# Moving GpSimd's elementwise work to VectorE, and projecting the pooling branch first, in a decoder step on one core

## The chip, the core and the metric

The kernel runs on one core of a Trainium2 chip, in one launch. The core's engines work side by side and wait for each other by semaphores: TensorE (PE in the profile; PEld is its loading of weights), VectorE (DVE), ScalarE (ACT), GpSimd (POOL) and SyncE (SP), which issues most of the DMAs. Each engine executes its own queue strictly in order, so an instruction that waits holds up everything behind it. The metric is the time of an execution in device microseconds; lower is better.

## The reference

Two layers work on 256 prompt tokens and 8 sample tokens (264 columns), with d = 1024. Each layer is a half-step feed-forward block, a mixer and a second half-step feed-forward block. Cut to what the change touches:

```python
def modulate(x, g, shift, scale):
    return rms_norm(x, g) * (1 + scale) + shift
def swiglu(h, w1, w2):
    gate, up = split(h @ w1);  return (silu(gate) * up) @ w2
def pool_mixer(u, ...):       # 4 channel groups of 64, windows w = 2, 4, 8, 16
    d = (c - c_prev) / min(w, pos + 1) - u          # c: running sums
    return concat(d @ pool_w[g]) * pool_scale
def merge_out(...):
    a = o.reshape(b, s, ATTN_WIDTH) @ w_oa          # attention branch, 768 wide
    p = pool_y @ w_op                               # pooling branch, 256 wide
    return (sigmoid(ga) * a + sigmoid(gp) * p) @ w_out
```

The 8 sample tokens attend to cached keys and values, 55 per head over three head groups, and that is done elementwise (multiply, then reduce), not on TensorE.

## The kernel before

**Exact products from a fast format.** Each weight and each activation is split into a high part in the fast format (`whi`, `h_hi`, `ah`) and the rest (`wlo`, `h_lo`, `al`). A block of 128x128 weights is three matmuls on 264 columns: high x high, low x high, high x low (`block`, `mm`, L495 to L508). ScalarE casts `whi`, VectorE subtracts to get `wlo`, in pieces of 128x512 for four blocks; at most some 24 blocks ahead of TensorE.

**Normalisation** (`norm_mod`, L461). After a stage's last product VectorE works out the row factors, scales eight chunks (`ht`, `h_scale`), ScalarE adds the shift and casts (`h_hi`, `h_shift`), and the low part is the difference (`h_lo`). Chunks 1, 3 and 5 (`ON_POOL`) get theirs on GpSimd in two operations, the other five on VectorE in one. The next stage's first two output chunks start in `mm_late` (L510): first the 32 matmuls that need `h_hi`, then the 16 that need `h_lo` (L521), those of GpSimd's chunks last. This happens five times after the start: before each mixer, and before each feed-forward block but the first.

**The mixer** (L592). 36 output chunks of the input projection run on TensorE; in between come the matmuls of attention. `prompt` does four rounds (two halves of the tokens, two head parities): scores into PSUM (`sc`, L779), biased on VectorE (`s`, L785), row maxima (`pnm`), exponentials on ScalarE, transposes, product with V (`oo`). `sample` does the 8 sample tokens: GpSimd multiplies the cached keys by q in four pieces (`kv`, L699), VectorE reduces; after the softmax GpSimd multiplies the values (L741), VectorE reduces into `os`; two masked copies `zo` go to TensorE (L755), whose result `oh`, `ol` completes the operands of the output projection. The pieces go through two buffers: piece i+2 is loaded by SyncE when piece i is reduced. `pooling` (L839) builds windowed sums on GpSimd (`sa`, `sb`) and three small operations for the samples on VectorE (`sm`).

**Order.** The program is written with a planner, class `Clock`: small generators (`spawn`) are resumed when the planned time, advanced by each block of TensorE's work (`tick`), reaches what they yield; `V.done()`, `A.done()` and `G.done()` are planned ends of an engine's queue, from a price per instruction that knows nothing of other engines. `clock.drain()` runs all that is left before the program goes on. So a change of engine changes the order in which TensorE's small matmuls stand among the large ones.

**Output** (L949). For each of eight chunks TensorE does 6 blocks of the attention branch (`pa`) and 2 of the pooling branch (`pp`), after the drain; VectorE multiplies each by its gate `tg`, GpSimd adds the two, ScalarE casts, GpSimd subtracts; then comes the product with `w_out`.

Of the kernel before, what the change touches and what calls it, by code (L numbers as in the profile page):

```python
# [18 lines left out]
KC = 8  # L19
# [15 lines left out]
          (61, 63, 65, 67, 69, 71, 73, 75), (95, 98, 101, 104, 107, 110, 113, 116), ())  # L35

ON_POOL = (1, 3, 5)

# [166 lines left out]
def decoder_step_kernel(ctx: ExitStack, tc: tile.TileContext, wts, ada0, ada, xin, first_in, consts_in, sel_in,  # L205
# [304 lines left out]
    def mm_late(chunks, ops):  # L510


        n = len(ops)
        held = []
        for k, (ah, al) in enumerate(ops):
            for ps, b in chunks:
                held.append((k in ON_POOL, k, ps, block(ps, b + k, ah, k == 0), al))

        held.sort(key=lambda v: v[:2])
        for _, k, ps, wh, al in held:  # L520
            nc.tensor.matmul(ps, wh, al, start=False, stop=(k == max(ON_POOL)))  # L521
        clock.tick(0.34 * n * len(chunks))
        return chunks[-1][1] + n
# [21 lines left out]
    def ffn(l, i, b, h, nxt):  # L545
        hh, hl = h
        with tc.tile_pool(name="ffn", bufs=1) as fp:
# [44 lines left out]
    def mixer(l, b, h):  # L592
# [82 lines left out]
        def sample():  # L675
# [60 lines left out]
            for i, (gs, s0, n) in enumerate(PIECES):  # L736
                yield from kv_wait()
                vv = kv.pop(0)[0].rearrange("p (d s) -> p d s", s=n)
                for g, a0, n_ in gs:
                    w = vv[:, :, a0:a0 + n_]  # L740
                    G.tensor_tensor(w, w, p55[:, s0 + a0:s0 + a0 + n_].unsqueeze(1).to_broadcast([P, 64, n_]),  # L741
                                            op=OP.mult)
                yield G.done()
                for g, a0, n_ in gs:
# [94 lines left out]
        def pooling():  # L839
# [3 lines left out]
            n = n16  # L843
            gp = G
            u = rows[:, 12:14]
            us = u[:, :, NP:NT]
            for i, w in enumerate((2, 4, 8, 16)):
# [3 lines left out]
            gp.memset(sa[:, :, 0:16], 0.0)  # L851
            gp.memset(sb[:, :, 0:16], 0.0)
            gp.tensor_copy(sa[:, :, 16:17], u[:, :, 0:1])
            gp.tensor_tensor(sa[:, :, 17:n], u[:, :, 1:NP], u[:, :, 0:NP - 1], op=OP.add)
            gp.tensor_tensor(sb[:, :, 16:n], sa[:, :, 16:n], sa[:, :, 14:n - 2], op=OP.add)
            gp.tensor_tensor(sa[:, 1, 16:n], sb[:, 1, 16:n], sb[:, 1, 12:n - 4], op=OP.add)
            gp.tensor_tensor(sb[64:, 1, 16:n], sa[64:, 1, 16:n], sa[64:, 1, 8:n - 8], op=OP.add)
            for c in range(2):
                for r, src in ((0, sa), (64, sb)):
                    cnt = cc[r:r + 64, C_CNT + c * 16:C_CNT + c * 16 + 16]  # L860
                    gp.tensor_tensor(sa[r:r + 64, c, 16:32], src[r:r + 64, c, 16:32], cnt, op=OP.mult)
                    gp.tensor_scalar(sa[r:r + 64, c, 32:n], src[r:r + 64, c, 32:n],
                                     cc[r:r + 64, C_IW + c:C_IW + c + 1], None, op0=OP.mult)
# [19 lines left out]
            clock.hold("sc", V)  # L883

        def start():
# [31 lines left out]
        for j in range(36):  # L917
# [23 lines left out]
            else:  # L941
                while j == 30 and st["scored"] < 4:
                    clock.tick(0.2)
                A.activation(tg[:, j - 20], ps, AF.Tanh, scale=0.5)
        clock.drain()
        ax.close()


        with tc.tile_pool(name="out", bufs=1) as op_:  # L949
# [3 lines left out]
            def merged(m):  # L953
                G.tensor_tensor(tg[:, m], tg[:, m], tg[:, 8 + m], op=OP.add)
                yield G.done()
                A.copy(mh[:, m], tg[:, m])
                yield A.done()
                G.tensor_tensor(ml[:, m], tg[:, m], mh[:, m].bitcast(F32), op=OP.subtract)

            for m in range(KC):  # L960
                pa = acc_tile()
                b = mm(pa, b, [(oh[:, k], ol[:, k]) for k in range(6)])
                pp = acc_tile()
                b = mm(pp, b, [(ph[:, k], pl[:, k]) for k in range(2)])
                V.scalar_tensor_tensor(tg[:, m], tg[:, m], 1.0, pa, op0=OP.add, op1=OP.mult)
                V.scalar_tensor_tensor(tg[:, 8 + m], tg[:, 8 + m], 1.0, pp, op0=OP.add, op1=OP.mult)
                clock.spawn(merged(m), V.done())
            mops = [(mh[:, k], ml[:, k]) for k in range(KC)]
# [122 lines left out]
def _constants():  # L1091
# [16 lines left out]
    for k in range(2):  # L1108
        for half in range(2):
            w = 2 ** (2 * k + half + 1)  # L1110
            cnt = np.minimum(w, np.arange(16) + 1)
            o = C_CNT + k * 16
            c[64 * half:64 * half + 64, o:o + 16] = (np.float32(1) / cnt.astype(np.float32))[None]
            c[64 * half:64 * half + 64, C_IW + k] = 1.0 / w
# [149 lines left out]
```

## Time and profile before

| What | Value |
|---|---|
| time, median of 3 runs | 1268.76 us (1268.53 to 1269.59) |
| the profiled execution | 1268.73 us, its span 1267.0 us |
| TensorE busy | 1240.2 us, 98% |
| VectorE, ScalarE, GpSimd busy | 809.8, 550.6, 207.0 us |
| mean granted clock of TensorE | 0.993 |
| chain that ended last | PE 91%, DVE 7% |

The span is the time from the first instruction to the last of one execution. TensorE's matmuls are pipelined and their ends are modelled, so "busy" covers small delays between matmuls; what a stage loses is read from the starts of its matmuls in the timeline. The granted clock is 1.00 at the higher of TensorE's two levels and 0.50 at the lower. Durations of neighbouring VectorE instructions overlap by some hundredths of a microsecond, so a run of them ends earlier than their sum.

### The profile page before, as it was taken

Reading aid. Unit: us, or ns where it says so; the run is one execution under the profiler, and the core shown is the slowest. Engines: PE = TensorE matmul, PEld = TensorE weight load, DVE = VectorE, ACT = ScalarE, POOL = GpSimd, SP = SyncE. Lnnn points to the kernel's source line nnn. Section 1 sums busy time; section 2 is a strip of 40 time slices with the busy share of each in tenths; the row PEclk is TensorE's granted clock in tenths of the full one; section 3 lists DMA queues with packets and bytes.
Section 4 is the critical chain, followed back from the end, with each engine's and each line's share of the span. In section 5 each row is a group of like instructions: output and inputs, shape, how many; then the busy total and the mean of one; then the engine's idle time right before and its main releaser. Section 6 shows DMA issues by size and latency. Waiting matters only on the chain.

```text
span 1267.0 us, 25911 instructions
## 1 busy us (share of the span) xinstructions
PE 1240.2 (98%) x10866; PEld 1176.0 (93%) x10866; DVE 809.8 (64%) x1533; ACT 550.6 (43%) x850; POOL 207.0 (16%) x218
## 2 busy tenths in 40 slices
PE   8999999999999999999999999999999999999998
PEld 6999999989899979999989999998997998999998
DVE  4555554676887775556567565557489878666653
ACT  2344333355453544344434444344555444544431
POOL 0012110010423321111002111001014251111100
PEclk9999999999898999999999999999999999999999
DMA  9688887555257737679745677763732784887652
GB/s 391 264 300 312 303 331 282 202 202 200 68 214 267 258 132 262 231 284 388 267 165 177 253 302 294 288 249 124 278 133 94 281 308 158 318 288 291 233 174 101
DMA packets 41989, 306.27 MB, mean 242 GB/s; under 512 B 4928, under 2 KB 6208, under 8 KB 8640
## 3 DMA queue, kind: packets, MB, share of 16 engines
q1 hardware_dynamic: 41248, 303.02, 64.8%
q8 instruction: 85, 1.39, 0.4%
q0 software_dynamic: 336, 1.29, 0.3%
q10 hardware_dynamic: 288, 0.30, 0.1%
q14 instruction: 32, 0.26, 0.1%
HBM read 299.73 MB, written 26.03 MB: 257 GB/s over the span
## 4 chain that ended last, share of the span: by engine, by line
PE 91%; DVE 7%; DMA 1%; issue 1%; ACT 0%; POOL 0%; DVEq 0%; SPq 0%; ACTq 0%; POOLq 0%
PE mm L497 27%; PE mm L498 26%; PE mm L506 26%; PE pa L286 3%; DVE ht L133 2%; PE mm L521 1%; PE oo L1072 1%; PE sc L779 1%; DMA wraw<-in_wts_dram 1%; DVE wlo L133 1%; DVE h_lo L133 1%; PE tr L807 1%; DVE sm L133 1%; PE oo L819 1%; PE pa L1012 1%
## 5 line engine op out<-in xcount | busy, mean ns | idle before, releaser
L133 DVE TENSOR_TENSOR wlo<-wraw,whi 128x512 fp32r<-128x512 f32 x736 | 547.5, 775 | 280.8 <-ACT whi L133 278.7
L497 PE MATMUL mm<-h_hi,whi 128*128 128x264 f32 x2088 | 600.9, 290 | 4.4 <-ACT h_hi L133 3.1
L133 ACT CAST whi<-wraw 128x1024 fp32r<-128x1024 f32 x368 | 384.8, 1049 | 489.1 <-PE mm L506 222.8
L498 PE MATMUL mm<-h_hi,wlo 128*128 128x264 f32 x2088 | 589.5, 284 | 0.0
L506 PE MATMUL mm<-h_lo,whi 128*128 128x264 f32 x1952 | 554.2, 284 | 0.0
L497 PEld LDWEIGHTS mm<-h_hi,whi 128*128 128x128 f32 x2088 | 394.7, 189 | 27.5 <-issue 15.8
L498 PEld LDWEIGHTS mm<-h_hi,wlo 128*128 128x128 f32 x2088 | 395.0, 189 | 0.0
L506 PEld LDWEIGHTS mm<-h_lo,whi 128*128 128x128 f32 x1952 | 367.3, 188 | 0.0
L498 PE MATMUL mm<-ah,wlo 128*128 128x264 f32 x704 | 201.1, 286 | 0.0
L506 PE MATMUL mm<-al,whi 128*128 128x264 f32 x704 | 200.2, 284 | 0.0
L497 PE MATMUL mm<-ah,whi 128*128 128x264 f32 x704 | 199.7, 284 | 0.0
L133 POOL TENSOR_TENSOR al<-fa,ah 128x264 fp32r<-128x264 f32 x88 | 89.6, 1019 | 495.3 <-ACT ah L133 494.0
L497 PEld LDWEIGHTS mm<-ah,whi 128*128 128x128 f32 x704 | 133.1, 189 | 2.5 <-issue 1.6
L498 PEld LDWEIGHTS mm<-ah,wlo 128*128 128x128 f32 x704 | 132.3, 188 | 0.0
L506 PEld LDWEIGHTS mm<-al,whi 128*128 128x128 f32 x704 | 132.1, 188 | 0.0
L133 DVE TENSOR_TENSOR fa<-fsi,mm 128x264 f32<-128x264 f32 x86 | 36.7, 427 | 71.1 <-PE mm L506 71.1
L133 POOL TENSOR_TENSOR ht<-ht,mods 128x256 f32<-128x256 f32 x15 | 11.1, 741 | 263.9 <-ACT h_hi L133 263.9
L133 ACT ACTIVATE h_hi<-ht,mods 128x256 fp32r<-128x256 f32 x48 | 22.6, 504 | 59.3 <-DVE ht L133 49.1
L133 DVE SCALAR_TENSOR_TENSOR x<-mm,mods,x 128x256 f32<-128x256 f32 x48 | 23.1, 481 | 39.4 <-PE mm L506 39.2
L286 PE MATMUL pa<-wraw,fc 128*32 128x256 f32 x544 | 36.4, 385 | 0.0
L133 ACT CAST ah<-fa 128x264 fp32r<-128x264 f32 x88 | 35.9, 409 | 0.6 <-DVE fa L133 0.6
L133 ACT ACTIVATE fsi<-mm 128x264 f32<-128x264 f32 x87 | 33.4, 383 | 0.5 <-PE mm L1036 0.3
(178 smaller groups left out, 947.9 us busy)
## 6 DMA issues: line engine op xcount, KB each, us to landing
wraw<-in_wts_dram SPq DMA_DIRECT2D x184, 1024.0 KB, 5.3
wraw<-in_ada_dram SPq DMA_DIRECT2D x34, 1024.0 KB, 5.8
araw<-in_ada_dram SPq DMA_DIRECT2D x30, 1024.0 KB, 7.3
a<-in_ada_dram SPq DMA_DIRECT2D x2, 2048.0 KB, 14.4
a<-in_ada_dram SPq DMA_DIRECT2D x4, 1024.0 KB, 22.4
out_og_dram<-in_cg_dram SPq DMA_DIRECT2D x2, 2032.0 KB, 10.4
out_rows_dram<-rows SPq DMA_DIRECT2D x2, 1848.0 KB, 10.8
kv<-in_ksamp_dram SPq DMA_DIRECT2D x8, 416.0 KB, 3.8
```

The source lines that it names most:

```text
L133: return f(*a, **k)
L286: nc.tensor.matmul(pa[32 * c:32 * c + 32], sc_t[:, 2 * q + r], t[:, r, c], start=(q + r == 0), stop=(q == 3 and r == 1), tile_position=(0, ...
L497: nc.tensor.matmul(ps, wh, ah, start=first, stop=False)
L498: nc.tensor.matmul(ps, wl, ah, start=False, stop=False)
L506: nc.tensor.matmul(ps, wh, al, start=False, stop=(k == n - 1))
L521: nc.tensor.matmul(ps, wh, al, start=False, stop=(k == max(ON_POOL)))
L779: nc.tensor.matmul(sc[e][:, i], qn[r:r + 64, c, q0:q0 + 128], rows[r:r + 64, c, 0:nk * 128], start=True, stop=True, tile_position=(r, 0))
L807: nc.tensor.transpose(pt[:, i], sf[:, k0:k0 + 128], ident)
L819: nc.tensor.matmul(po[64 * e:64 * e + 64, g], st["vt"][:, kt, h_ * 64:h_ * 64 + 64], s[e][:, g, kt * 128:kt * 128 + 128], start=(kt == 0), ...
L1012: nc.tensor.matmul(pa[32 * c:32 * c + 32], sc_t[:, r], t[:, r, c], start=(r == 0), stop=(r == KC - 1), tile_position=(0, 32 * c))
L1072: nc.tensor.matmul(pw, wr[:, 0:P], wr[:, 0:n], start=True, stop=True)
```

## The change

All two-tensor operations of GpSimd go to VectorE: the low parts of the three chunks in the normalisation (now the same one operation as the others; `mm_late` has no late chunks any more), the low parts `al` in the feed-forward blocks, the multiplications of the sample's keys and values, the windowed sums, and the merge of the branches. GpSimd keeps memsets and a few DMAs. Pooling multiplies by 1/w and subtracts the token in one operation; the counts of the first 16 positions are scaled by w to fit. The eight `pp` chunks are computed ahead of the drain, right after the input projection, and the weights lie in that order; after the drain come the eight `pa` chunks.

```diff
@@ norm_mod
-            if m in ON_POOL:
-                G.tensor_tensor(ts[m], ts[m], mods[l][:, 3 * i, m, 0:1].to_broadcast([P, NP]), op=OP.add)
-                G.tensor_tensor(lo[:, m, 0:NP], ts[m], hi[:, m, 0:NP].bitcast(F32), op=OP.subtract)
         next(smp, None)
-        for m in [m for m in range(KC) if m not in ON_POOL]:
+        for m in range(KC):
             h_low(l, i, m, hi, lo, ts[m])
@@ mm_late
-                held.append((k in ON_POOL, k, ps, block(ps, b + k, ah, k == 0), al))
-
-        held.sort(key=lambda v: v[:2])
-        for _, k, ps, wh, al in held:
...
+                held.append((k, ps, block(ps, b + k, ah, k == 0), al))
+        for k, ps, wh, al in held:
...
@@ gated
                 A.copy(ah[:, c], a)
-                G.tensor_tensor(al[:, c], a, ah[:, c].bitcast(F32), op=OP.subtract)
+                yield A.done()
+                V.tensor_tensor(al[:, c], a, ah[:, c].bitcast(F32), op=OP.subtract)
@@ sample (keys; the values change alike)
-                    G.tensor_tensor(kk[:, a0:a0 + n_], kk[:, a0:a0 + n_],
+                    V.tensor_tensor(kk[:, a0:a0 + n_], kk[:, a0:a0 + n_],
                                             sqkv[:, g].unsqueeze(1).to_broadcast([P, n_, 64]), op=OP.mult)
-                yield G.done()
+                yield V.done()
@@ pooling
+            V.tensor_tensor(sa[:, :, 17:n], u[:, :, 1:NP], u[:, :, 0:NP - 1], op=OP.add)
+            yield V.done()
+            V.tensor_tensor(sb[:, :, 16:n], sa[:, :, 16:n], sa[:, :, 14:n - 2], op=OP.add)
+            yield V.done()
...
+            for c in range(2):
+                for r, src in ((0, sa), (64, sb)):
...
+                    V.tensor_tensor(src[r:r + 64, c, 16:32], src[r:r + 64, c, 16:32], cnt, op=OP.mult)
+                    V.scalar_tensor_tensor(sa[r:r + 64, c, 16:n], src[r:r + 64, c, 16:n],
+                                           cc[r:r + 64, C_IW + c:C_IW + c + 1], u[r:r + 64, c, 0:NP],
+                                           op0=OP.mult, op1=OP.subtract)
+                yield V.done()
...
-            gp.tensor_tensor(sa[:, :, 16:n], sa[:, :, 16:n], u[:, :, 0:NP], op=OP.subtract)
-            yield G.done()
@@ mixer, output
+        while not st.get("pool"):
+            clock.tick(0.2)
+        for m in range(KC):
+            pp = acc_tile()
+            b = mm(pp, b, [(ph[:, k], pl[:, k]) for k in range(2)])
+            V.scalar_tensor_tensor(tg[:, 8 + m], tg[:, 8 + m], 1.0, pp, op0=OP.add, op1=OP.mult)
         clock.drain()
...
-                G.tensor_tensor(tg[:, m], tg[:, m], tg[:, 8 + m], op=OP.add)
-                yield G.done()
+                V.tensor_tensor(tg[:, m], tg[:, m], tg[:, 8 + m], op=OP.add)
+                yield V.done()
...
-                G.tensor_tensor(ml[:, m], tg[:, m], mh[:, m].bitcast(F32), op=OP.subtract)
+                V.tensor_tensor(ml[:, m], tg[:, m], mh[:, m].bitcast(F32), op=OP.subtract)
...
-                pp = acc_tile()
-                b = mm(pp, b, [(ph[:, k], pl[:, k]) for k in range(2)])
...
-                clock.spawn(merged(m), V.done())
+                clock.spawn(merged(m))
+                clock.run(clock.t)
```

What the planner makes of it is read from the order of the instructions. First VectorE in the normalisation, before:

```order
L133 SCALAR_TENSOR_TENSOR ht<-x,mods,rb 128x256 x7
L133 TENSOR_TENSOR hs<-hs,mods 128x64
L133 TENSOR_TENSOR h_lo<-hs,h_hi 128x8x8
L133 SCALAR_TENSOR_TENSOR h_lo<-ht,mods,h_hi 128x256 x5
L133 STREAM_TRANSPOSE tt<-pa 128x256
```

and now:

```order
L131 SCALAR_TENSOR_TENSOR ht<-x,mods,rb 128x256 x7
L131 TENSOR_TENSOR hs<-hs,mods 128x64
L131 TENSOR_TENSOR h_lo<-hs,h_hi 128x8x8
L131 SCALAR_TENSOR_TENSOR h_lo<-ht,mods,h_hi 128x256 x8
L131 STREAM_TRANSPOSE tt<-pa 128x256
```

Three `h_lo` join the five, and nothing else moves there. Next VectorE in the attention of layer 0, from the scores of the third round (`s`, the first four of six) to those of the fourth, before:

```order
L133 SCALAR_TENSOR_TENSOR s<-cc,sc 128x256 x4
L133 TENSOR_TENSOR of<-oo,of 128x384
L133 TENSOR_TENSOR wlo<-wraw,whi 128x512
L133 TENSOR_TENSOR sm<-sm,rows 128x16
L133 TENSOR_TENSOR sm<-sm,cc 128x16
L133 TENSOR_TENSOR sa<-sm,rows 128x2x8
L133 SCALAR_TENSOR_TENSOR s<-cc,sc 128x256 x2
L133 TENSOR_REDUCE pnm<-s 128x1 x2
L133 TENSOR_REDUCE s_4048<-kv 128x13
L133 SCALAR_TENSOR_TENSOR s<-cc,sc 128x256 x4
```

and now:

```order
L131 SCALAR_TENSOR_TENSOR s<-cc,sc 128x256 x4
L131 TENSOR_TENSOR sa<-sb 128x256
L131 TENSOR_TENSOR sb<-sa 64x256
L131 TENSOR_REDUCE s_4030<-kv 128x13
L131 TENSOR_TENSOR kv<-kv,sqkv 128x832
L131 TENSOR_TENSOR of<-oo,of 128x384
L131 TENSOR_TENSOR wlo<-wraw,whi 128x512
L131 SCALAR_TENSOR_TENSOR s<-cc,sc 128x256 x2
L131 TENSOR_REDUCE pnm<-s 128x1 x2
```

The three small `sm` operations stand later now, and sums, a reduction and a multiplication stand in their place; on TensorE the fourth round's scores come after 27 large matmuls behind the third's last scores, where 6 stood before. Last TensorE at the end of the sample's attention, before:

```order
L498 MATMUL mm<-h_hi,wlo 128x264
L506 MATMUL mm<-h_lo,whi 128x264
L755 MATMUL tr<-cc,zo 128x16 x3
L497 MATMUL mm<-h_hi,whi 128x264
L498 MATMUL mm<-h_hi,wlo 128x264
```

and now:

```order
L493 MATMUL mm<-ph,wlo 128x264
L501 MATMUL mm<-pl,whi 128x264
L749 MATMUL tr<-cc,zo 128x16 x3
L492 MATMUL mm<-oh,whi 128x264
L493 MATMUL mm<-oh,wlo 128x264
```

The transposes of `zo` stand behind the 48 matmuls of the pooling branch now, and directly ahead of the attention branch, which reads their result; two blocks of the input projection stood between before.

## Rows read from the trace of the kernel before

**Rows 1.** The page, busy time of each engine over the whole span.
```profile
PE 1240.2 (98%) x10866; PEld 1176.0 (93%) x10866; DVE 809.8 (64%) x1533; ACT 550.6 (43%) x850; POOL 207.0 (16%) x218
```

**Rows 2.** Waits of TensorE: us in total, times, longest.
```profile
PE sc L779 <- DVE s L133: 6.2, 2, 3.1
PE tr L755 <- DVE zo L133: 4.1, 2, 2.2
```

**Rows 3.** Timeline of one normalisation: start, us, engine, operation, count, wait in brackets.
```profile
254.30 0.48 DVE L133 SCALAR_TENSOR_TENSOR ht<-x,mods,rb 128x256 f32<-128x256 f32 x1
...
254.81 1.85 ACT L133 ACTIVATE h_hi<-ht,mods 128x256 fp32r<-128x256 f32 x4 [4.88 <-DVE ht L133]
254.83 4.54 DVE L133 SCALAR_TENSOR_TENSOR ht<-x,mods,rb 128x256 f32<-128x256 f32 x7
...
255.37 0.39 PE L497 MATMUL mm<-h_hi,whi 128*128 128x264 f32 x1 [0.55 <-ACT h_hi L133]
...
255.93 0.64 POOL L133 TENSOR_TENSOR ht<-ht,mods 128x256 f32<-128x256 f32 x1 [69.36 <-ACT h_hi L133]
...
260.67 2.06 DVE L133 SCALAR_TENSOR_TENSOR h_lo<-ht,mods,h_hi 128x256 fp32r<-128x256 f32 x5
...
261.19 2.84 PE L521 MATMUL mm<-h_lo,whi 128*128 128x264 f32 x16 [0.48 <-DVE h_lo L133]
```

**Rows 4.** VectorE's groups by shape: busy us, mean ns, idle before.
```profile
L133 DVE TENSOR_TENSOR wlo<-wraw,whi 128x512 fp32r<-128x512 f32 x736 | 547.5, 775 | 280.8 <-ACT whi L133 278.7
...
L133 DVE SCALAR_TENSOR_TENSOR ht<-x,mods,rb 128x256 f32<-128x256 f32 x48 | 28.5, 651 | 0.0
...
L133 DVE SCALAR_TENSOR_TENSOR tg<-tg,mm 128x264 f32<-128x264 f32 x32 | 13.7, 427 | 7.0 <-PE mm L506 6.9
L133 DVE SCALAR_TENSOR_TENSOR s<-cc,sc 128x256 f32<-128x256 f32 x24 | 8.6, 410 | 3.7 <-PE sc L779 3.7
L133 DVE TENSOR_REDUCE s<-kv 128x13 f32<-128x832 f32 x8 | 8.1, 1006 | 0.0
...
L133 DVE TENSOR_REDUCE o<-kv 128x64 f32<-128x576 f32 x2 | 1.5, 742 | 0.0
```

**Rows 5.** Timeline of the score stall, layer 0; the last row is layer 1.
```profile
332.28 1.13 PE L779 MATMUL sc<-rows,tg 64*128 64x256 f32 x8
...
336.43 4.31 POOL L133 TENSOR_TENSOR kv<-kv,sqkv 128x832 f32<-128x832 f32 x2
...
336.94 1.94 DVE L133 TENSOR_TENSOR sm<-sm,rows 128x16 f32<-128x16 f32 x1
...
337.52 0.28 PE L498 MATMUL mm<-h_hi,wlo 128*128 128x264 f32 x1
...
338.01 0.28 PE L506 MATMUL mm<-h_lo,whi 128*128 128x264 f32 x1
341.37 2.40 PE L779 MATMUL sc<-rows,tg 64*128 64x256 f32 x8 [3.08 <-DVE s L133]
...
961.25 2.37 PE L779 MATMUL sc<-rows,tg 64*128 64x256 f32 x8 [3.08 <-DVE s L133]
```

**Rows 6.** Windows: us, busy PE, PEld, DVE, ACT, POOL (count), granted clock, DMA, GB/s.
```profile
340.00:344.00 4.00, 2.63 (x9) 1.98 (x10) 3.97 (x7) 1.40 (x3) 0.74 (x1) 0.55 0.00 0
```

**Rows 7.** Windows of TensorE alone: us, busy (count), granted clock, DMA, GB/s.
```profile
347.00:348.00 1.00, 1.00 (x9) 0.88 1.06 427
401.00:402.00 1.00, 1.00 (x7) 0.57 0.98 418
965.00:966.00 1.00, 1.00 (x10) 0.97 0.83 113
```

**Rows 8.** The key and value tiles: time from issue to landing.
```profile
DMA to landing us min/median/max: 3.3/3.7/7.3
```

**Rows 9.** Timeline where the sample's result reaches TensorE, layers 0 and 1.
```profile
394.78 1.26 PE L755 MATMUL tr<-cc,zo 128*128 128x16 f32 x6 [2.23 <-DVE zo L133]
...
1013.34 0.84 PE L755 MATMUL tr<-cc,zo 128*128 128x16 f32 x6 [1.90 <-DVE zo L133]
```

More of the change, by code (lines that the diff above doesn't have):

```diff
@@ L35 @@
           (61, 63, 65, 67, 69, 71, 73, 75), (95, 98, 101, 104, 107, 110, 113, 116), ())
-ON_POOL = (1, 3, 5)
 FIRST = ((0, 4), (4, 6), (6, 8))
@@ L516, in mm_late @@
             for ps, b in chunks:
-                held.append((k in ON_POOL, k, ps, block(ps, b + k, ah, k == 0), al))
-        held.sort(key=lambda v: v[:2])
-        for _, k, ps, wh, al in held:
-            nc.tensor.matmul(ps, wh, al, start=False, stop=(k == max(ON_POOL)))
+                held.append((k, ps, block(ps, b + k, ah, k == 0), al))
+        for k, ps, wh, al in held:
+            nc.tensor.matmul(ps, wh, al, start=False, stop=(k == n - 1))
         clock.tick(0.34 * n * len(chunks))
@@ L740, in sample @@
                     w = vv[:, :, a0:a0 + n_]
-                    G.tensor_tensor(w, w, p55[:, s0 + a0:s0 + a0 + n_].unsqueeze(1).to_broadcast([P, 64, n_]),
+                    V.tensor_tensor(w, w, p55[:, s0 + a0:s0 + a0 + n_].unsqueeze(1).to_broadcast([P, 64, n_]),
                                             op=OP.mult)
-                yield G.done()
+                yield V.done()
                 for g, a0, n_ in gs:
@@ L843, in pooling @@
             n = n16
-            gp = G
             u = rows[:, 12:14]
             us = u[:, :, NP:NT]
+            G.memset(sa[:, :, 0:16], 0.0)
+            G.memset(sb[:, :, 0:16], 0.0)
+            A.copy(sa[:, :, 16:17], u[:, :, 0:1])
+            V.tensor_tensor(sa[:, :, 17:n], u[:, :, 1:NP], u[:, :, 0:NP - 1], op=OP.add)
+            yield V.done()
+            V.tensor_tensor(sb[:, :, 16:n], sa[:, :, 16:n], sa[:, :, 14:n - 2], op=OP.add)
+            yield V.done()
+            V.tensor_tensor(sa[:, 1, 16:n], sb[:, 1, 16:n], sb[:, 1, 12:n - 4], op=OP.add)
+            V.tensor_tensor(sb[64:, 1, 16:n], sa[64:, 1, 16:n], sa[64:, 1, 8:n - 8], op=OP.add)
+            yield V.done()
+            for c in range(2):
+                for r, src in ((0, sa), (64, sb)):
+                    cnt = cc[r:r + 64, C_CNT + c * 16:C_CNT + c * 16 + 16]
+                    V.tensor_tensor(src[r:r + 64, c, 16:32], src[r:r + 64, c, 16:32], cnt, op=OP.mult)
+                    V.scalar_tensor_tensor(sa[r:r + 64, c, 16:n], src[r:r + 64, c, 16:n],
+                                           cc[r:r + 64, C_IW + c:C_IW + c + 1], u[r:r + 64, c, 0:NP],
+                                           op0=OP.mult, op1=OP.subtract)
+                yield V.done()
             for i, w in enumerate((2, 4, 8, 16)):
@@ L850, in pooling @@
                                         axis=AX.X, op=OP.add)
[L851 to L863, printed above, removed]
-            gp.tensor_tensor(sa[:, :, 16:n], sa[:, :, 16:n], u[:, :, 0:NP], op=OP.subtract)
-            yield G.done()
             V.tensor_tensor(sm, sm, us, op=OP.add)
@@ L883, in pooling @@
             clock.hold("sc", V)
+            st["pool"] = True
         def start():
@@ L953, in merged @@
             def merged(m):
-                G.tensor_tensor(tg[:, m], tg[:, m], tg[:, 8 + m], op=OP.add)
-                yield G.done()
+                V.tensor_tensor(tg[:, m], tg[:, m], tg[:, 8 + m], op=OP.add)
+                yield V.done()
                 A.copy(mh[:, m], tg[:, m])
                 yield A.done()
-                G.tensor_tensor(ml[:, m], tg[:, m], mh[:, m].bitcast(F32), op=OP.subtract)
+                V.tensor_tensor(ml[:, m], tg[:, m], mh[:, m].bitcast(F32), op=OP.subtract)
             for m in range(KC):
@@ L962, in mixer @@
                 b = mm(pa, b, [(oh[:, k], ol[:, k]) for k in range(6)])
-                pp = acc_tile()
-                b = mm(pp, b, [(ph[:, k], pl[:, k]) for k in range(2)])
                 V.scalar_tensor_tensor(tg[:, m], tg[:, m], 1.0, pa, op0=OP.add, op1=OP.mult)
-                V.scalar_tensor_tensor(tg[:, 8 + m], tg[:, 8 + m], 1.0, pp, op0=OP.add, op1=OP.mult)
-                clock.spawn(merged(m), V.done())
+                clock.spawn(merged(m))
+                clock.run(clock.t)
             mops = [(mh[:, k], ml[:, k]) for k in range(KC)]
@@ L1112, in _constants @@
             o = C_CNT + k * 16
-            c[64 * half:64 * half + 64, o:o + 16] = (np.float32(1) / cnt.astype(np.float32))[None]
+            c[64 * half:64 * half + 64, o:o + 16] = (np.float32(w) / cnt.astype(np.float32))[None]
             c[64 * half:64 * half + 64, C_IW + k] = 1.0 / w
@@ L1183 @@
                 stream.append(tiles(blocks(a["w_in"][l], (2, 0, 1, 3))))
-                both = np.concatenate([a["w_oa"][l], a["w_op"][l]], axis=0)
-                stream.append(tiles(blocks(both, (2, 0, 1, 3))))
+                stream.append(tiles(blocks(a["w_op"][l], (2, 0, 1, 3))))
+                stream.append(tiles(blocks(a["w_oa"][l], (2, 0, 1, 3))))
                 stream.append(tiles(blocks(a["w_out"][l], (2, 0, 1, 3))))
```

## The prediction

> **What bounds the kernel now.** I read the page's busy times first: TensorE is busy for 1240.2 of 1267.0 us [rows 1]. So an edit on another engine counts only where TensorE waits for that engine, and the next view is the list of TensorE's waits. Two of its lines are long: the scores `sc` of L779 wait for VectorE's `s`, 3.1 us in each layer, and the transposes of L755 wait for `zo`, 2.2 us at most [rows 2]. The third place hides inside "busy": in the timeline of a normalisation the first pass begins at 255.37 and the second ends at 264.03 [rows 3]. That is 48 matmuls, and a matmul follows the one before by 0.12 us where nothing is in the way (four of them from 337.52 to 338.01 [rows 5]), so 5.8 us of work take 8.5. There are five such places. Of this only what GpSimd's work causes can go.
>
> GpSimd slows VectorE. The first `ht` of the normalisation starts at 254.30 and the next at 254.83 with a small operation between, but seven take 4.54 us, 0.65 each, and they stretch once GpSimd begins at 255.93 [rows 3]; the mean of all 48 is 651 ns, while `s`, as many elements from PSUM and SBUF in the same kind of instruction, takes 410 [rows 4]. It is starker in the attention: `sm`, on 16 elements per partition, takes 1.94 us beside two GpSimd multiplications of 2.15 each [rows 5].
>
> **The change part by part.** All sums are against the profiled execution's 1268.73 us, 1.7 more than its span and practically the median of the runs, 1268.76.
>
> *A, normalisation.* It adds three `h_lo` per place and takes GpSimd away. After the change: seven `ht` from 254.83 at 0.41 (the price of `s`) end at 257.7; two small operations, 0.4 together; eight `h_lo` at 0.41 each, as five take 2.06 when GpSimd has finished [rows 3], end at 261.4. TensorE is through its first pass earlier: 32 matmuls from 255.37, at most one group of four per ScalarE's 0.46 (four in 1.85 [rows 3]) or per 4 x 0.12, whichever is longer, end by 259.4. So the last `h_lo` decides, and with 0.1 us to the two last matmuls and their modelled end of 0.28 the place ends at 261.9 instead of 264.0: 2.1 us. Five times: -10.5. Ends: had the 0.65 nothing to do with GpSimd, the last `h_lo` would come 1.2 us later than now and the six matmuls for GpSimd's chunks (0.7) would no longer trail, +0.5 a place or +2.5; were `ht` as quick as the rows' overlap allows, -12.5.
>
> *B, scores.* Before, the first eight `sc` take 1.13 us [rows 5]; the stalled ones wait 3.08 and take 2.40, since the granted clock stands at 0.55 in 340 to 344 [rows 6]. It comes back at about 347.2 (0.88 in the window from 347 [rows 7]), so the stretch from 343.7 to there, 3.5 us at half the speed, loses 1.8 more. Layer 0 loses 3.08 + 1.27 + 1.8 = 6.1; layer 1 3.08 + 1.24 and, with the clock back at 965.06, half of 1.5: 5.1. After: TensorE reaches these scores at 332.28 + 1.13 + 15 x 0.12 + 0.6 (the third round's last scores, half as many) + 27 x 0.12 + 1.2 (transposes and `oo`: some 19 matmuls of 128 columns, an estimate at half of 0.12) = 340.2. VectorE needs, from the third round's first scores at 333.4: 4 x 0.41, two sums 0.8, a reduction 1.0 and a multiplication as wide 1.0, `of` 0.55 (384 elements, between the 410 ns of 256 and the 742 of 576), a `wlo` 0.78 at most, two `s` 0.8 [rows 4]: 339.9, and some 0.5 less as they overlap. So the wait goes, by a margin of 0.3 to 0.8 us. -11.2; ends 0 (a stall as long elsewhere in the layer) and -11.2.
>
> *C, end of the sample.* Before: 2.23 us of wait, 0.4 on the slowed transposes and half of the 6.0 us to about 401.9 where the clock returns [rows 7, 9], 5.6 in layer 0; layer 1 waits 1.90 and keeps its clock: 7.5 together. After, 48 matmuls of the pooling branch (5.85 us from a point S) stand ahead of the transposes. They look like a cover, but VectorE has no time either. A `wlo` depends on a cast whose buffer TensorE frees, so VectorE can't run ahead, and from the first gate product at about S + 0.8 it has in its queue ahead of the end of `zo`: 7 gate products at 0.43, 3 `wlo` at 0.78, the multiplication and the reduction of the last piece (0.74 + 0.41 each, after the reduction of 576 elements [rows 4] and `s`), and four small ones, an estimate of 0.3 each, below the 0.41 of 256 elements: 8.8, or S + 9.6. The overlap of some 0.07 on 16 operations takes off 1.1: S + 8.5. TensorE is done at S + 6.2: of three accumulators the sixth product needs the one that the third gate product frees at about S + 4.0 (0.8 + 3 x 0.43 + 0.78 + 1.15), and would start at S + 3.65. So it idles 2.3 us again, and 0.55 more because `oh` and `ol` are read at once, with no two blocks between. The clock fell after 2.23 and not after 1.90 [rows 7, 9]; I take one fall of 3.0 us: (2.3 + 0.3 + 0.55) x 2 + 3.0 = 9.3, so +1.8. Ends: no idle, 1.1 - 7.5 = -6.4; 3.4 us of idle with two falls, +7.0.
>
> *At nothing: the feed-forward blocks.* 88 `al` at 0.43 join VectorE. A chunk there is 16 blocks or 48 matmuls, 5.8 us; VectorE needs four `wlo` (3.1), `fa` and `al` (0.9): 4.0. The second product reads the last `al` only in its 22nd block, 8 us on. Without that cover it is 0.5 us a block of feed-forward, four times.
>
> *At nothing: pooling and merge.* Pooling costs VectorE about 4.5 us a layer (two operations of 512 elements at 0.7, six of 256 at 0.41, four of 16 at an estimated 0.2), and by the order its product comes on TensorE 102 large matmuls, 12 us, after the scores above; the merge is one more operation of 0.43 and one subtraction per 18 matmuls. Cover gone, the last merge (1.7 us from product to cast) would show, but `mm_late` reads that chunk only after 28 matmuls, 3.4 us.
>
> *The waits that are added.* The key and value multiplications now wait for their DMAs in VectorE's queue, with scores and `wlo` behind them. A load lands 3.7 us after its issue, 7.3 at most [rows 8], and by the order VectorE has eight or more other operations, some 6 us, between the reduction that frees the buffer and the multiplication. Nothing by the median, 1.3 us by the maximum.
>
> Sum: -10.5 - 11.2 + 1.8 = -19.9, or 1248.8; I say 1249.
>
> VectorE is busy for 3.97 of 4 us while TensorE stalls [rows 6]. The Trainium skill, in "Perfetto Trace Analysis", section "Optimizing Scalar/DVE Operations", says that with a saturated VectorE it may make sense to offload, even to GpSimd, which speaks against this change; the same place warns that the two share a read port and that moving work between them might not help. By the first half the time would be that of the third rival below; the 1.94 us for 16 elements speak for the second half, since much of that 3.97 is waiting.
>
> **The rivals.**
> 1. *The sample is through in time.* The pooling branch hides `zo`, C is -6.4: 1268.7 - 10.5 - 11.2 - 6.4 = 1240.6. For it: 5.85 us of cover. Against: my count of VectorE's queue, unless the operations overlap more.
> 2. *A new stall of the same kind.* The score stall goes, but a round's maxima, or a key multiplication, comes late elsewhere in each layer and brings the clock down: B is nothing, 1260. For it: a margin below 1 us, which one `wlo` more uses up. Against: without GpSimd the planner's prices are near what VectorE takes.
> 3. *VectorE's queue becomes the bound (slower).* Place: the attention, from the first key multiplication to `zo`. It gains eight pieces at 1.0 (as the reductions [rows 4]) and 4.5 of pooling, 12.5 us a layer. If nothing comes back from GpSimd there and VectorE has no slack, TensorE waits for all of it, 25 us: 1268.7 - 10.5 + 25 = 1283. It decides from the point where VectorE lags by more than the 24 blocks, 8.8 us, that `wlo` is ahead. Against: operations of microseconds for 16 elements shrink to 0.2.
> 4. *GpSimd isn't what stretches `ht`.* A is +2.5: 1261.8. Against: the first `ht`.
> 5. *No change.* A and B come only by half and the sample's end costs its upper 7.0: 1268.7 - 5 - 5.6 + 7 = 1265, or with one more stall about 1268.
>
> **How the numbers follow.** Forecast 0.58; rivals in order 0.14, 0.13, 0.07, 0.04, 0.04. The range of 8 in 10 goes from the first rival's time to the second's, 1240 to 1260; the forecast's own is 1244 to 1254. A measurement tells 0.2%, about 2.5 us, from no change. Faster: 0.58 + 0.14 + 0.13 + 0.04 = 0.89; the same 0.04; slower 0.07.
>
> **What the profile after would show.** Right: `ht` at some 0.41 us in the mean; the last matmul of the second pass 6.5 us after the first of the first pass instead of 8.7; no wait of `sc` for `s` in the list, and no low clock there; a wait of the transposes for `zo` of about 2 us in each layer, behind the pooling branch. VectorE's `wlo` shorter than 775 ns. Wrong: `ht` still near 0.65 (then A falls); a wait over 2 us of a `sc`, `tr` or `oo` in the attention; no wait for `zo` (then C was too dear); waits of large matmuls for `wlo` (then the third rival).

## The result and the profile after

The changed kernel takes 1251.76 us (median of 4 runs, 1250.90 to 1252.62), the kernel before 1268.64 beside it: ratio 0.9870, interval 0.9853 to 0.9887. The forecast was 1249, its range 1240 to 1260. The profiled execution took 1250.9 us, span 1249.1.

The page's first lines, to be read beside [rows 1]: GpSimd is all but empty (4.1 us), and VectorE's 1716 instructions, 88 `al` among them, take less time than before.

```profile
span 1249.1 us, 25734 instructions
...
PE 1230.0 (98%) x10866; PEld 1170.8 (94%) x10866; DVE 787.7 (63%) x1716; ACT 548.5 (44%) x852; POOL 4.1 (0%) x16
```

TensorE's waits (total, times, longest), beside [rows 2]: the line of `sc` is gone, that of `zo` has grown, and two short ones are new, for an accumulator (`tg`: its gate product on VectorE frees it) and for `oh`.

```profile
PE tr L749 <- DVE zo L131: 5.0, 2, 2.5
PE mm L492 <- ACT h_hi L131: 3.2, 5, 0.8
...
PE mm L492 <- DVE tg L131: 0.9, 2, 0.5
PE mm L492 <- ACT oh L131: 0.6, 2, 0.3
```

The normalisation of [rows 3]: `ht` runs through, and the second pass no longer waits for `h_lo`.

```profile
254.50 2.86 DVE L131 SCALAR_TENSOR_TENSOR ht<-x,mods,rb 128x256 f32<-128x256 f32 x7
...
257.67 3.25 DVE L131 SCALAR_TENSOR_TENSOR h_lo<-ht,mods,h_hi 128x256 fp32r<-128x256 f32 x8
...
255.04 0.39 PE L492 MATMUL mm<-h_hi,whi 128*128 128x264 f32 x1 [0.56 <-ACT h_hi L131]
259.12 2.37 PE L514 MATMUL mm<-h_lo,whi 128*128 128x264 f32 x16
```

VectorE's groups by shape (busy us, mean ns, idle before), beside [rows 4]: `ht` 651 to 479 ns, `wlo` 775 to 687; `s`, which has one operand in PSUM, stays where it was (410, now 416).

```profile
L131 DVE TENSOR_TENSOR wlo<-wraw,whi 128x512 fp32r<-128x512 f32 x736 | 488.9, 687 | 288.1 <-ACT whi L131 285.7
...
L131 DVE SCALAR_TENSOR_TENSOR ht<-x,mods,rb 128x256 f32<-128x256 f32 x48 | 20.1, 479 | 0.0
...
L131 DVE SCALAR_TENSOR_TENSOR s<-cc,sc 128x256 f32<-128x256 f32 x24 | 8.6, 416 | 2.1 <-PE sc L773 2.1
...
L131 DVE TENSOR_TENSOR sm<-sm,rows 128x16 f32<-128x16 f32 x2 | 0.4, 176 | 0.1
```

The scores of the fourth round, stalled in [rows 5], start without a wait: VectorE's two `s` of the third round, which these scores wait for, end at 337.3, and TensorE comes at 338.94. Counted from the third round's first scores (332.28 before, 330.24 now), the two `s` start after 6.3 us and not 8.6, and TensorE comes after 8.7 us, where it would have come after 6.0 (341.37 less its wait of 3.08). First VectorE before, then the changed kernel:

```profile
340.90 0.74 DVE L133 SCALAR_TENSOR_TENSOR s<-cc,sc 128x256 f32<-128x256 f32 x2
```

```profile
330.24 1.14 PE L773 MATMUL sc<-rows,tg 64*128 64x256 f32 x8
...
336.57 0.74 DVE L131 SCALAR_TENSOR_TENSOR s<-cc,sc 128x256 f32<-128x256 f32 x2
...
338.94 1.14 PE L773 MATMUL sc<-rows,tg 64*128 64x256 f32 x8
```

The window of [rows 6] is full, at full clock.

```profile
340.00:344.00 4.00, 4.00 (x35) 3.99 (x34) 3.99 (x9) 1.99 (x5) 0.00 (x0) 1.00 0.26 57
```

The end of the sample, beside [rows 9]: VectorE first (from 386.77 on, seven gate products `tg` stand ahead of the last reductions and `zo`), then TensorE, which begins the pooling branch at 385.26, has finished it by 392 and waits in both layers.

```profile
386.77 0.76 DVE L131 SCALAR_TENSOR_TENSOR tg<-tg,mm 128x264 f32<-128x264 f32 x2
...
391.62 0.42 DVE L131 SCALAR_TENSOR_TENSOR tg<-tg,mm 128x264 f32<-128x264 f32 x1
391.95 0.75 DVE L131 TENSOR_REDUCE o<-kv 128x64 f32<-128x576 f32 x1
...
393.71 0.73 DVE L131 TENSOR_SCALAR zo<-os,cc 128x192 f32<-128x192 f32 x2
...
385.26 0.28 PE L492 MATMUL mm<-ph,whi 128*128 128x264 f32 x1
...
389.53 0.39 PE L492 MATMUL mm<-ph,whi 128*128 128x264 f32 x1 [0.47 <-DVE tg L131]
...
394.49 0.84 PE L749 MATMUL tr<-cc,zo 128*128 128x16 f32 x6 [2.50 <-DVE zo L131]
395.62 0.48 PE L492 MATMUL mm<-oh,whi 128*128 128x264 f32 x1 [0.29 <-ACT oh L131]
...
1002.40 0.84 PE L749 MATMUL tr<-cc,zo 128*128 128x16 f32 x6 [2.51 <-DVE zo L131]
```

Windows of TensorE alone behind these waits (busy, granted clock, DMA, GB/s): the lower level, 1.2 GHz, in both layers; at this place the kernel before had it in layer 0 alone ([rows 7]).

```profile
396.00:399.00 3.00, 3.00 (x16) 0.50 0.91 289
...
1004.00:1006.00 2.00, 2.00 (x11) 0.50 0.86 233
```

The loads of [rows 8] land in 3.4 us at the median, 6.5 at most, and nothing waits for them.

### The profile page after: what moved, and what is told of

The parts are those of the page before. It is cut to its first block, busy times and chain, and to the rows that moved or that the text cites. A ratio compares the mean times of both kernels' runs of the same rounds, so it can differ in the third digit from the quotient of the medians.

```text
span 1249.1 us, 25734 instructions
## 1 busy us (share of the span) xinstructions
PE 1230.0 (98%) x10866; PEld 1170.8 (94%) x10866; DVE 787.7 (63%) x1716; ACT 548.5 (44%) x852; POOL 4.1 (0%) x16
## 3 DMA queue, kind: packets, MB, share of 16 engines
q8 instruction: 85, 1.39, 0.5%
## 4 chain that ended last, share of the span: by engine, by line
PE 94%; DVE 4%; issue 0%; ACT 0%; POOL 0%; DVEq 0%; ACTq 0%; POOLq 0%
PE mm L492 29%; PE mm L493 28%; PE mm L501 26%; PE pa L284 3%; PE oo L1074 1%; PE mm L514 1%; PE sc L773 1%; PE oo L813 1%; PE tr L801 1%; PE pa L1014 1%; DVE wlo L131 1%; DVE ht L131 1%; DVE h_lo L131 0%; DVE tg L131 0%; DVE o L131 0%
## 5 line engine op out<-in xcount | busy, mean ns | idle before, releaser
L131 DVE TENSOR_TENSOR wlo<-wraw,whi 128x512 fp32r<-128x512 f32 x736 | 488.9, 687 | 288.1 <-ACT whi L131 285.7
L131 DVE TENSOR_TENSOR al<-fa,ah 128x264 fp32r<-128x264 f32 x88 | 37.5, 427 | 0.0
L492 PE MATMUL mm<-oh,whi 128*128 128x264 f32 x96 | 28.9, 301 | 0.6 <-ACT oh L131 0.6
```

The costliest lines, as they stand in the source:

```text
L131: return f(*a, **k)
L492: nc.tensor.matmul(ps, wh, ah, start=first, stop=False)
```

## The experiments

Times are medians; a difference is against the kernel before of the same job (1267.8 to 1268.7 us), or against the changed kernel where said.

**1. The normalisation alone, in the kernel before.**

```
-ON_POOL = (1, 3, 5)
+ON_POOL = ()
-  ... stop=(k == max(ON_POOL)))
+  ... stop=(k == n - 1))
```

> The kernel before with one edit: the low parts of all eight chunks of the normalisation on VectorE (all else as before). Theory (GpSimd's six operations stretch VectorE's there): each of five places takes 6.4 us from the first matmul to the end of the second pass instead of 8.6, ht falls from 651 to about 480 ns, and the time falls by 11 us, to 1257.7. Rival (ht is as slow by itself, so VectorE only gets three operations more): +2.5 us, 1271. The score stall and the waits for zo stay as before under both.

1257.82 us (ratio 0.9928, 0.9915 to 0.9942): 10.4 less. `ht` 479 ns, `wlo` still 775, the wait for `s` as before, those for `zo` 3.1 us in all and not 4.1. Term A stands by itself, at its predicted price.

**2. The changed kernel with GpSimd's six normalisation operations as extra work** on a tile that nothing reads; VectorE's and TensorE's queues hold the same instructions in the same order.

```
+ if m in (1, 3, 5):
+     G.tensor_tensor(sh[:, 0], ts[m], shift, op=OP.add)
+     G.tensor_tensor(sh[:, 1], sh[:, 0], hi[m], op=OP.subtract)
```

> The changed kernel, with GpSimd doing the six operations of the normalisation of before once more into a tile that nobody reads; VectorE's and TensorE's queues are the same, instruction by instruction. Theory (contention with GpSimd): ht goes back to about 650 ns, each of the five places takes 9 us or more instead of 6.4, and the time rises by 13 us, to 1265. Rival (the gain came from the order of the instructions or from no longer waiting for GpSimd's results): nothing waits for the tile, so the time stays within 1 us of 1251.8.

1266.24 us, 14.5 more than the changed kernel. In the timeline `ht` is back at its old pace though nobody waits for GpSimd:

```profile
254.85 4.55 DVE L131 SCALAR_TENSOR_TENSOR ht<-x,mods,rb 128x256 f32<-128x256 f32 x7
255.65 0.95 POOL L131 TENSOR_TENSOR shadow<-ht,mods 128x256 f32<-128x256 f32 x1 [252.99 <-ACT h_hi L131]
...
260.69 3.25 DVE L131 SCALAR_TENSOR_TENSOR h_lo<-ht,mods,h_hi 128x256 fp32r<-128x256 f32 x8
261.21 3.07 PEld L518 LDWEIGHTS mm<-h_lo,whi 128*128 128x128 f32 x16 [0.69 <-DVE h_lo L131]
```

So GpSimd's mere activity stretches `ht`; rival 4 is out. From the first matmul to the end of the second pass the five places take 45.1 us together instead of 32.0, which is 13.1 of the 14.5 us. That is more than A because eight `h_lo`, not five, now follow the stretched `ht`.

**3. The changed kernel with extra GpSimd work in the attention**: five additions of 384 elements behind each key multiplication, unread.

```
+ G.tensor_tensor(sh, kk[:, 0:6], fc, op=OP.add)
+ for _ in range(4): G.tensor_tensor(sh, sh, fc, op=OP.add)
```

> The changed kernel, with five GpSimd additions of 384 elements behind each of the four key multiplications, into a tile that nobody reads; VectorE's and TensorE's queues are unchanged. GpSimd is then busy for some 5 us behind each piece, about as it was around the score stall before. Theory (the stall of 3.1 us came from VectorE being held by GpSimd): VectorE's two-input operations there stretch again to over 1 us each, the third round's last s end 1.5 us or more later, the 1.7 us that VectorE is now ahead of the fourth round's scores goes, a wait of TensorE for s comes back (up to 3 us a layer), and the time rises by 2 to 10 us. Rival (the planner now puts 27 large matmuls ahead of these scores instead of 6, and that removed the stall): no wait of sc, time within 1.5 us of 1251.8.

1260.68 us, 8.9 more than the changed kernel. Waits for `s` (1.9 us, two) and for the pooling's `sa` (2.7) appear, and those for an accumulator grow from 0.9 to 3.0. By shape, the same operations on VectorE: 64x256 at 1108 and 892 ns (422 and 477 in the changed kernel), 64x16 at 458 (158).

```profile
L131 DVE SCALAR_TENSOR_TENSOR sa<-sa,cc,rows 64x256 f32<-64x256 f32 x4 | 3.6, 892 | 0.1
L131 DVE TENSOR_TENSOR sb<-sa 64x256 f32<-64x256 f32 x2 | 2.2, 1108 | 0.1
...
L131 DVE TENSOR_TENSOR sa<-sa,cc 64x16 f32<-64x16 f32 x4 | 1.8, 458 | 0.0
```

The waits for `s` came at the fourth round's second scores, not at its first, where the kernel before had stalled. There VectorE's two `s` start 8.2 us after the third round's first scores (330.26), almost as late as before (8.6), and TensorE still does not wait (its scores take 1.39 us and not 1.14):

```profile
338.43 0.74 DVE L131 SCALAR_TENSOR_TENSOR s<-cc,sc 128x256 f32<-128x256 f32 x2
...
338.96 1.39 PE L777 MATMUL sc<-rows,tg 64*128 64x256 f32 x8
```

So GpSimd's activity alone makes VectorE late again and costs 8.9 us, but at the old stall's own place the new order, with 27 large matmuls in front of the scores and not 6, is by itself cover enough. The rival is right about that place and wrong about the time.

**4. The changed kernel with the old order of the output** (drain first, `pa` and `pp` in turn).

> The changed kernel with the output projection in the old order: after the drain, and pa and pp in turn, weights laid out accordingly; all work of GpSimd stays on VectorE. Theory (the pooling branch covers most of the sample's longer queue on VectorE, at the price of its gate products standing in that queue): TensorE waits about 4.5 us for zo in each layer instead of 2.5, the wait for an accumulator (0.5) and for oh (0.3) goes, the lower clock lasts longer, together +3 to +6 us: 1255 to 1258. Rival (the order is worth nothing, since the gate products take what the cover gives): within 1 us of 1251.8.

1254.71 us, 3.0 more than the changed kernel; TensorE waits 4.3 us for `zo` in each layer instead of 2.5.

**5. The order alone, in the kernel before.**

```
+ while not st.get("pool"): clock.tick(0.2)
+ for m in range(KC):  pp = ...; gate product      # ahead of the drain
  clock.drain()
```

> The kernel before with the output's order alone changed: the pooling branch's eight projections stand ahead of the drain, so that they run while the end of the sample's attention is worked out; every two-tensor operation stays on GpSimd. Theory: in the kernel before, zo is there about 4.6 us after TensorE has run out of w_in's products, and the eight projections take about 5.9 us, so both waits for zo (3.1 us on average, two of them) go, and only the hand-over of oh and ol (about 0.5 us per layer) is new: 6.4 us less than the kernel before, 1262 us. Rival: the values' multiplications on GpSimd come so late that TensorE still waits behind the projections, as it does in the changed kernel (2.5 us): 1267 to 1269 us.

1267.42 us (ratio 0.9997, 0.9982 to 1.0011): nothing, the rival's number. But not for the rival's reason: in the trace the transposes of `zo` (at 393.22, behind a wait of 1.33 us) stand ahead of all pooling products, and so they do in layer 1 (1.60 us). The pooling on GpSimd ends so late in the planner's time that the `while` runs the sample through to `zo` first. The cover was never in place.

**6. The changed kernel, loads held for less of the planner's time.**

```
-  kv.append((kv_load(...), clock.t + 6.0))
+  kv.append((kv_load(...), clock.t + 4.0))
```

> The changed kernel with one number of the planner altered: after it has asked for a piece of the keys or values, it holds the work on that piece back for 4.0 us of its clock and not 6.0 (the transfer lands 3.7 us after its issue at the median). Theory: the change's loss at the end of the sample's attention is one of order, since the last multiplications by the values stand too late in VectorE's list, behind all eight gate products; with 4.0 zo stands behind three gate products, is there about 4 us earlier, and the waits for zo (2.5 us) and the two falls of TensorE's clock (about 1.5 us each) go, against up to 0.7 us of a longer wait for an accumulator: 3 to 4 us less per layer, 1244 to 1246 us. Rival: VectorE as such is full at this place, or the transfer has not landed: within 1.5 us of the changed kernel's 1251.8 us, or slower.

1251.28 us: no difference, the rival's number. The wait for `zo` is gone, as the theory had it, but its place is taken by one for an accumulator, whose gate product now stands behind `zo`:

```profile
392.00 0.39 PE L492 MATMUL mm<-ph,whi 128*128 128x264 f32 x1 [1.56 <-DVE tg L131]
```

VectorE is all but full there (12.3 of the 13 us from 381 to 394), so its order only chooses who waits. In layer 0 the clock fell all the same (0.59 in 393 to 395); in layer 1, after the same 1.56 us, it didn't.

**7. The changed kernel with `al` back on GpSimd.**

> The changed kernel with the 88 subtractions of the feed-forward gate (al) given back to GpSimd, all else as changed. Theory: on VectorE they cost nothing, as TensorE is not waiting for VectorE in the feed-forward stages; given back they only make VectorE's wlo operations longer again (from 687 ns toward 775 ns): within 1 us of 1251.8 us. Rival: the 38 us that they take on VectorE push other work late, or the yield put in for them does: 1249 to 1250 us, 2 us faster.

1251.86 us, 0.1 from the changed kernel, with `wlo` at 748 ns. Nothing, as predicted: 60 ns on each of 736 `wlo` are 44 us of VectorE that no one waits for.

**8. The changed kernel with the multiplications by keys and values back on GpSimd.**

> The changed kernel with the multiplications by keys and values given back to GpSimd (64 to 832 elements each, in 5 pieces of keys and 5 of values per layer), all else as changed: normalisation and pooling stay on VectorE. Theory: what held up the scores in the kernel before is GpSimd's long multiplication beside VectorE's operations on two SBUF operands, so VectorE's pooling and weight splits lie under it again and the wait of TensorE for s comes back at least in part (1.0 to 3.1 us per layer), while the end of the sample's attention is no earlier than in the changed kernel: 1254 to 1258 us. Rival: the scores were held up by GpSimd's own pooling alone, which VectorE waited for; then the wait for s stays away, VectorE has about 10 us less to do per layer before the end, and the kernel is as fast as the changed one or faster: 1247 to 1252 us.

1253.87 us, 2.1 more than the changed kernel. Within 0.2 us of the theory's lower end, but not by its way: no wait for `s` came back. TensorE waits instead for the sample's exponentials (2.1 and 1.9 us), `sqkv`, `sa` and, in layer 1, an accumulator (1.7), and not for `zo`.

**9. The pooling alone on VectorE, in the kernel before** (`sa` and `sb` in fused steps, all else as before).

> The kernel before with the pooling branch alone on VectorE in its fused steps; normalisation, keys, values, feed-forward and the output's order stay as before. Theory: the wait of TensorE for the scores (3.1 us and a fall of its clock, in each layer) came from VectorE's sm, which stood behind GpSimd's pooling and in front of s; with the pooling on VectorE it goes, though GpSimd's multiplications by the keys still slow VectorE beside them, which gives a part back: 4 to 9 us less than before, 1259 to 1264 us. Rival: the wait came from GpSimd's multiplications by the keys, which hold up VectorE's operations on two SBUF operands whoever does the pooling; with 16 us more on VectorE the scores are as late or later: 1267 us or more, with the waits for s still there.

1271.76 us (ratio 1.0029, 1.0013 to 1.0044): 3.9 *slower*; my theory fell. The wait for `s` has gone, as it said, and what took its place costs more. TensorE's waits:

```profile
PE tr L726 <- ACT s L133: 4.0, 2, 2.1
PE tr L755 <- DVE zo L133: 3.6, 2, 1.8
...
PE tr L807 <- DVE sqkv L133: 2.2, 2, 1.1
PE sc L877 <- DVE sa L133: 2.0, 2, 1.1
```

and behind the first of them the clock is low (0.77 in 373 to 378). It falls four times, after the waits for the exponentials and for `zo` in both layers, where it fell three times before. Part of this is GpSimd beside VectorE: two `wlo` ahead of the `sqkv` that is waited for take 4.21 us, and the key multiplications now lie beside the pooling and stretch it, 16 elements to 0.90 us and 256 to 1.35:

```profile
323.20 4.21 DVE L133 TENSOR_TENSOR wlo<-wraw,whi 128x512 fp32r<-128x512 f32 x2
...
341.94 0.90 DVE L133 TENSOR_TENSOR sb<-sb,cc 64x16 f32<-64x16 f32 x1
342.87 1.35 DVE L133 SCALAR_TENSOR_TENSOR sa<-sb,cc,rows 64x256 f32<-64x256 f32 x1
```

But the longest wait, for the exponentials (`s` on ScalarE), is not VectorE's: on ScalarE they stand behind a weight cast (`whi`) that waits 2.78 us for its load and starts at 369.61; in layer 1 that is 2.53 us, and in experiment 8 it is 2.72 and 2.55. Why the load is late there no run isolates; SyncE's order has changed too. The rival had the time, not the place: it expected the waits for `s` to stay.

**10. As 6, with `zo` on ScalarE.**

```
-  V.tensor_scalar(zo[:, :, e], os, mask, None, op0=OP.mult)
+  A.activation(zo[:, :, e], os, AF.Copy, scale=mask)
```

> The changed kernel with the loads held for 4.0 us instead of 6.0, and zo's two products (0.73 us on VectorE together) on ScalarE. Theory: at the end of the sample's attention VectorE is full from 381 to 394 us and whatever stands late in its list is waited for; with the loads held for 4.0 us that is the gate product behind zo (TensorE waits 1.56 us for an accumulator), and 0.65 us less of VectorE's work in front of it leaves a wait of about 0.9 us: 0.5 to 1.5 us less over both layers than with zo on VectorE (1251.3 us), 1250 to 1251 us. Rival: ScalarE is itself late there, and zo on it brings the wait for zo back: 1251.5 us or more.

1247.47 us (1246.84 to 1247.84; ratio 0.9840, 0.9822 to 0.9857): faster than both kernels, 4.3 below the changed one and 3.8 below number 6, where 0.5 to 1.5 below number 6 was expected. The accumulator's wait is down to 0.80, as expected; what the theory had left out is that the clock now holds. Its mean is 1.000 in all four executions, and in number 6 from 0.995 (1252.0 us) to 0.999 (1248.35). Windows as above:

```profile
391.19 0.39 PE L492 MATMUL mm<-ph,whi 128*128 128x264 f32 x1 [0.80 <-DVE tg L131]
```

```profile
396.00:399.00 3.00, 3.00 (x27) 1.00 1.01 423
...
1004.00:1006.00 2.00, 2.00 (x19) 1.00 0.97 410
```

In layer 0 a part comes back later: TensorE waits at the merge 0.62 us for `tg` and 1.2 in front of the product with `w_out`.

**11 and 12. Pooling with the new order; pooling with keys and values.** Both in the kernel before; they show whether the parts add up.

> The kernel before with the pooling on VectorE and the new order of the output; normalisation, keys and values, feed-forward and merge stay on GpSimd. Theory: the new order hides the wait for zo only where the pooling branch's result is there before the planner reaches the end of the sample; with GpSimd's pooling it wasn't (the order alone moved nothing), with VectorE's it is: the waits for zo (3.6 us with the pooling alone) and what they cost in the clock go, 5 to 8 us less than the pooling alone (1271.8 us): 1264 to 1267 us. Rival: the two parts simply add up (+3.9 and -0.4 us): 1270 to 1272 us.

1265.42 us (ratio 0.9974, 0.9964 to 0.9983): 3.3 less than before. The parts alone give +3.9 and -0.4, so together they are 6.8 better than their sum: with VectorE's pooling, five of the eight products (ten of the 16 blocks) do stand ahead of `zo`, and nothing waits for `zo`; an accumulator is waited for instead, 0.48 and 1.57 us.

> The kernel before with the pooling and the multiplications by keys and values on VectorE; normalisation, feed-forward, merge and the output's order stay as before. Theory: the scores' gain needs both moves: with the pooling alone TensorE waits elsewhere (for exp, sqkv and sa) because GpSimd's key multiplications are late and slow VectorE; with the keys on VectorE these waits go and the wait for s does not come back, while the wait for zo grows to about 4 us in each layer, as in the changed kernel with the old order (1254.7 us, from which this one differs by the normalisation's 10.4 us): 1264 to 1266 us. Rival: the pooling alone was slower because VectorE has more to do, and the keys and values add 8 us per layer to that: 1272 us or more.

1265.32 us (ratio 0.9975, 0.9964 to 0.9986): 3.4 less than before, 7.3 better than with the pooling alone. No wait for `s`, the exponentials, `sqkv` or `sa`; the one for `zo` is 4.3 us in each layer. With the normalisation's 10.4 and the order's 3.0 this makes 1252, the changed kernel. On this base the parts add up, within intervals of 1 to 2 us for each. The keys and values alone, with the pooling left on GpSimd, were not run.

## Why the prediction was right, and where it was off

The mechanism was the predicted one and the time came 2.1 us over the sum (1248.8 against the profiled 1250.9). By its steps:

- **A, -10.5.** From the first matmul to the end of the second pass the five places take 6.45, 6.32, 6.44, 6.44 and 6.32 us, where they took 8.66, 8.50, 8.63, 8.64 and 8.53: -11.0 together, and -10.4 in experiment 1. Right; `ht` follow each other at 0.41, as taken from `s`, though each is listed with 0.48.
- **B, -11.2.** The end of `w_in`, counted from the third round's first scores (332.28 before, 330.24 now), comes 5.8 us sooner in layer 0 and 4.8 in layer 1: -10.6. (Before, two of its blocks stand behind the transposes of `zo`; they are counted without that wait.) No wait and no low clock, as said, with a margin of 1.6 us instead of 0.3 to 0.8, since TensorE comes 8.7 us after that round's first scores and not 7.9, VectorE 7.1 as summed. The way from a stall of 3.1 to that margin is two things: VectorE is 2.3 us sooner and, by the new order, TensorE 2.7 us later. Either alone would have left less than 1 us of the stall (an estimate: 3.08 - 2.3 and 3.08 - 2.7), and experiment 3 shows the place without a stall by the order alone. Both are in the sum, where the order is the 27 x 0.12. Experiment 9 takes this stall away and gains nothing, since TensorE then waits elsewhere; 12 shows that B comes with pooling, keys and values together, and whether keys and values would do alone is open. For the whole change the term holds; for its parts it would have misled.
- **C, +1.8.** This is the mis-sized term. By the starts of the matmuls the place loses 7.6 us before (7.5 in the sum) and 10.8 now, not 9.3: +3.2. The failing step is "from the first gate product at about S + 0.8". The queue from there to the end of `zo` takes 7.7 us, as counted, but VectorE comes to it only at S + 1.5 (386.77 against 385.26), since reductions and a `wlo` of the piece before still stand in front. So `zo` is there at S + 9.2 and not 8.5, and TensorE loses 0.7 us for the accumulator (0.3) and 2.6 for `zo` (2.3); `oh` costs 0.4 (0.55). "I take one fall of 3.0 us" is wrong too and cost nothing, by luck: the clock fell in both layers, by 1.6 us each. Together (2.6 + 0.7 + 0.4 + 1.6) x 2 = 10.6 of the 10.8.
- **At nothing.** `al` costs nothing (experiment 7). The waits for loads cost nothing. That the pooling and the merge hide holds in the changed kernel; the pooling does not hide beside GpSimd's multiplications (experiment 9).
- **Not foreseen**, together about +0.5: a wait of 0.24 us for `wlo` behind the first mixer's normalisation and one of 0.25 for the sum of squares, probably because TensorE now comes sooner.

With these the steps give -11.0 - 10.6 + 3.2 + 0.5 = -17.9, and the profiled executions differ by 17.8. That the time came so near the sum is in part luck: A fell 0.5 us more than said, B 0.6 less.

The rivals: the first (`zo` in time) is wrong, by VectorE's queue, as counted. Experiment 10 removes the wait for `zo` and the falls of the clock and comes to 1247.5, still 7 us above that rival's 1240.6. The second's mechanism exists (experiment 3) and did not set in. The third names the right engine at the end of the sample, with 2.5 us a layer and not 12.5.

The Trainium skill says in "Perfetto Trace Analysis", section "Optimizing Scalar/DVE Operations", that with a saturated VectorE it may make sense to offload, even to GpSimd. Here that would have misled: VectorE looked full beside GpSimd (3.97 of 4 us), and with all of GpSimd's two-tensor work on it, it is busy for 787.7 us and not 809.8, its `wlo` alone 59 us less. The same section of the Trainium skill warns that the two share a read port, so that moving work between them might not help. Experiment 2 agrees with the port, as GpSimd's unread work brings `ht` from 479 back to 653 ns. By "SBUF — State Buffer" of the Trainium skill, section "Who interferes with whom", a VectorE operation with two SBUF inputs contends with GpSimd's reads, and a reduction on this chip doesn't. The traces agree: `ht` is stretched, the `s` that reads PSUM is not (410 and 416 ns), and a reduction of 832 elements takes 1.02 us beside GpSimd's additions (334.86 in experiment 3) and 1016 ns without them.

## What to carry to other kernels

Where VectorE's operations on two SBUF operands take several times their usual time, look at what GpSimd does in the same microseconds before calling VectorE saturated: moving that work *onto* VectorE can leave it with less to do. Where a planner orders every engine's queue, moves don't add up part by part (pooling +3.9, order -0.4, both -3.3; pooling with keys and values -3.4), so price the whole set, and read the new order of all queues, ScalarE's and SyncE's too. When a full engine makes another wait, reordering its queue only changes who waits; taking 0.7 us off it, to an engine that is free at that moment, was worth more than the wait itself, since TensorE's clock then held.

## What was not expected of the hardware

TensorE's clock fell after idle gaps of 2.50 and 2.51 us (changed kernel), 2.13, 1.88 and twice 1.82 (experiment 9), 1.60 (experiment 5, layer 1) and 1.56 (experiment 6, layer 0). It did not fall after the same 1.56 in layer 1 of experiment 6, after 1.90 in [rows 9], nor after 2.04 in layer 1 of experiment 11. So the length of a gap alone doesn't say it, and a gap near 2 us has to be priced with and without a fall (by the starts of the matmuls 1.6 us in each layer of the changed kernel, 2.8 in layer 0 of the kernel before).

The contention reaches some operations with a single large SBUF input too. `os` multiplies 64 elements by a per-partition scalar; beside GpSimd's value multiplications it took 1339 ns, without them 250. But `z`, also a multiplication by a per-partition scalar, on 96 elements, kept its 0.24 us beside a GpSimd addition (326.87 in the kernel before); what sets the two apart no run shows. Groups by shape, first of the kernel before, then of the changed one:

```profile
L133 DVE TENSOR_SCALAR os<-sqkv,p 128x64 f32<-128x64 f32 x6 | 7.7, 1339 | 0.1
```

```profile
L131 DVE TENSOR_SCALAR os<-sqkv,p 128x64 f32<-128x64 f32 x6 | 1.2, 250 | 0.1
```
